# Who makes the sums of the output weights in a Strassen-Winograd feed-forward block: VectorE or GpSimd

## The chip, the cores and the metric

The kernel runs on one core of a Trainium2 chip. The metric is the device time of one execution in microseconds (us). The kernel before takes 2497.96 us, the median of three runs (2496.34 to 2498.91).

In the views of the profile the engines are called PE (TensorE, the matmuls), PEld (its weight loads), DVE (VectorE), ACT (ScalarE), POOL (GpSimd) and SP (SyncE, which here only issues DMAs). PEq, SPq and the like are the sequencers of those engines. Each engine takes its instructions strictly in the order in which they stand in its queue: an instruction that waits holds up all that stand behind it on the same engine.

## The reference

Two layers of an encoder trunk over 1024 prompt tokens and 32 tokens of a running stream, model width 1024, feed-forward width 2816, all in fp32. Layer 0 mixes tokens by a gated linear recurrence (HGRN2), layer 1 by attention over a sliding window. Behind each mixer stands a SwiGLU block with a norm on both sides:

```python
x = x + rms_norm(mix, norm_mix_post[layer])
hf = rms_norm(x, norm_ffn_pre[layer])
a, b = jnp.split(hf @ w_ffn_in[layer], 2, axis=-1)
x = x + rms_norm((jax.nn.silu(a) * b) @ w_ffn_out[layer], norm_ffn_post[layer])
```

The change lies in the last line of it, in the product with `w_ffn_out` and in what is prepared for it while the product with `w_ffn_in` runs.

## The kernel before, in words

Tokens stand in three blocks: block 0 and block 1 of 384 columns, block 2 of 288. Every fp32 product is made of three matmuls on halves in fp32r: a weight tile `wst` arrives by DMA from SP's queue (L91, 512 KB), ACT casts it to the high half `wh` (L102), DVE subtracts to get the low half `wl` (L103), and PE adds high by high, high by low and low by high. There are two buffers for `wst`, so that SP can have a unit's two tiles under way and no more.

**The up projection** (`ffn`, the loop over `j`) has 22 units of 256 output features. Units 0 to 3 are plain. Units 4 to 21 are `fin_7(j)`: for blocks 0 and 1 a Strassen-Winograd scheme with seven products in place of eight, 12 matmuls of 384 columns each (L520), and for block 2 plain products in two halves, 24 matmuls of 288 columns each (`fin_half`, L142); the last two units leave block 2 to later. At the head of a unit `prep(j)` makes four sums of the unit's two weight tiles (L463 to L465, `sr`, `sh`, `sl`), and in it DVE joins the products: `u` is the sum of the first two (L554, called u2 below; it is also what frees the PSUM bank that the second half of block 2 takes), `uk` two further ones, kept in four buffers. SP stores the outcome to `g` in HBM (L380, L570, L576). After each second unit `tpart` makes four sums of activations, and POOL's queue stores them to `t` (L501).

**The sums for the down projection.** The output weights stand in HBM in quarters `wo[0]` to `wo[3]`. `spart(c)` takes a strip of 384 columns of all four (the last strip is 256 wide), and there are 15 strips, called pieces below. Per piece POOL's queue loads four tiles of 192 KB (L484), DVE makes four sums (L485 to L488), and POOL's queue stores them to `sd` (L490). The four tiles have the tags `xo` (two of them, two buffers), `rb2` and `nv` (one buffer each); so a piece's loads wait until the stores of the piece before have landed. The loop asks for piece 0 at unit 5, for the second `tback` (sums of activations of units 0 to 3) at unit 6, and for one piece per unit after that; a scheduler then sets the order on each engine, and since POOL's rows wait for no matmul, its pieces follow each other as fast as they can from unit 6 on.

**The norm's loads.** Behind the last piece the tag `xo` belongs to the norm of the next stage: its loads of the residual stream (L292, `xo<-xsa` in layer 0, `xo<-xsc` in layer 1) stand in SP's queue between the weight loads of the last units, and take the buffers that the pieces use.

**The down projection** runs through a list `PR` of products; each loads six weight tiles (five of 512 KB, one of 256 KB) and the activations to them (L647 and the load ahead of it, tiles `gl` and `gh`), and multiplies (L679). A product can carry a third block along on the same weight tiles (`third`). Between groups of matmuls a table (`s0`, `s1` in `hook`) says how many steps of the norm of block 0 and block 1 are taken. In layer 1 the kernel ends with `put2` for block 2, a sum over partitions on PE (L245, L262) and the last four vector operations (L828, L829) before the output is stored.

Of the kernel before, what the change touches and what calls it, by code (L numbers as in the profile page):

```python
# [8 lines left out]
F32 = mybir.dt.float32  # L9
# [50 lines left out]
def build(nc, tc, I, O):  # L60
# [281 lines left out]
    def ffn(L, nx, post1, post, wmix, v1, w2, xold, wnext, spill, yout, res):  # L342
# [135 lines left out]
        def spart(c):  # L478

            n = slice(c * 384, min(c * 384 + 384, NP2 * 512))  # L480
            w = n.stop - n.start
            a11, a12, a21, a22 = ts = four(w)
            for i, t in enumerate(ts):
                nc.gpsimd.dma_start(t, wo[i][:, n])  # L484
            nc.vector.tensor_tensor(a22, a21, a22, add)  # L485
            nc.vector.tensor_tensor(a21, a11, a21, sub)
            nc.vector.tensor_tensor(a11, a22, a11, sub)
            nc.vector.tensor_tensor(a12, a12, a11, sub)  # L488
            for i, t in enumerate((a22, a11, a21, a12)):
                nc.gpsimd.dma_start(sd[i][:, n], t)  # L490
# [90 lines left out]
        for j in range(NSTD, NF):  # L581
            if j in (NSTD, NSTD + 2):
                tback((j - NSTD) // 2)
            elif pieces:
                spart(pieces.pop(0))
            fin_7(j, j < NF - 2)
        close(spc)
# [38 lines left out]
        if yout is None:  # L626
            PR = [p + (None,) for p in (P1, P6, P2, P7, P4, P5, P3, (A11, E), (A12, F), (A22, F), (A21, E))]
        else:
            PR = [P1 + (E,), P2 + (F,), P6 + (None,), P7 + (None,), P4 + (F,), P5 + (None,), P3 + (None,),
                  (A21, E, None)]  # L630
# [84 lines left out]
        def put2(k, x, more):  # L715

            d = dst(k, 2)
            if yout is None:
                put(k, 2, lambda d: tt_(d, d, x, add) if more else nc.scalar.copy(d, x))
                return None  # L720

            if more:
                tt_(d, d, x, add)
                x = d
            if k < KT - 1:
                sq_acc(accs[2], W, x, k == 0)
                q = None
            else:
                q = tmp()
                nc.scalar.activation(q[:, :W], x, AF.Square)  # L730
            nc.scalar.activation(d, x, AF.Copy, scale=pcol(w2, k))
            return q

        if yout is None:
# [29 lines left out]
            for h in range(2):  # L764
# [5 lines left out]
                for m in M:  # L770
                    put2(4 * h + m, pt[m][:, :W], False)
        else:
# [5 lines left out]
            for m in M:  # L778
                put(m, 0, lambda d: nc.scalar.copy(d, pb[m][:, :384]))
                put2(m, pa[m][:, :W], False)  # L780
# [8 lines left out]
            pb = four_b()  # L789
            product(pa, 384, False, third=(pb, True, True))  # L790
            for m in M:
                put(4 + m, 0, lambda d: tt_(d, Y[:, m, :], pa[m][:, :384], add))
                nc.scalar.copy(dst(4 + m, 2), pb[m][:, :W])

            s0 = {1: 1, 2: 1, 3: 1, 4: 1, 6: 1, 8: 1}
            s1 = {11: 1, 12: 2, 13: 1, 14: 2}
            pa = four_a()
            side[0] = True
            product(pa, 384, True, hook(0, (0, s0)))
            for m in M:  # L800
                put(4 + m, 1, lambda d: tt_(d, d, pa[m][:, :384], add))
            product(pa, 384, False, hook(5, (0, s0)))
            for m in M:
                put(m, 1, lambda d: tt_(d, Y[:, m, :], pa[m][:, :384], add))
            if yout is not None:

                xo = newx(0)[0].bitcast(F32)[:, :, :W]
                nc.sync.dma_start(xo, xold[2])
            pb = four_b()
            side[0] = False  # L810
            product(pb, W, True, hook(10, (0, s0), (1, s1)))
            for m in M:
                q = put2(4 + m, pb[m][:, :W], True)
# [1002 lines left out]
```

## Time and profile before

| what | value |
|---|---|
| median of three runs | 2497.96 us |
| the profiled execution's own time | 2498.63 us |
| its span (first to last instruction in the trace) | 2496.9 us |
| mean granted clock of TensorE | 0.987 |
| busy: PE, DVE, ACT, POOL | 2391.6, 1821.6, 1163.1, 432.6 us |
| units 4 to 21 of layer 0 | 728.0 to 1111.0 us |
| units 4 to 21 of layer 1 | 1837.5 to 2224.0 us |
| down projection of layer 0 | 1123.7 to 1378.7 us |
| down projection of layer 1 | 2236.5 to 2474.3 us |

How to read the views: the first part of the page gives the busy time of each engine and its share of the span. A row of the groups names the line, engine, operation and tiles, then how often, the busy time in us and the mean of one in ns, and behind the last bar how long the engine sat idle just before, and what ended that (`<-`). A row of the timeline begins with the start and the length in us; in brackets stands the idle time before it and its releaser. A row of the windows has, for one stretch, its length and each engine's busy time in us with the number of instructions, then PE's granted clock, the share of time of the DMA engines and GB/s.

### The profile page before, as it was taken

To read this page: it belongs to the slowest core of one execution; us is meant where nothing else is said; L and a number is where in the kernel's file an instruction comes from. 1 tells how busy PE (TensorE), PEld (TensorE's weight loads), DVE (VectorE), ACT (ScalarE), POOL (GpSimd) and SP (SyncE) were. 2 spreads that over 40 slices of the span, in tenths; PEclk is the share of its full clock that TensorE was granted. 3 is DMA by queue.
4 is the path that set the end of the run, shared out by engine and by line. 5 is a ranking of instruction groups with operands and counts; after the bars stand their busy time and mean duration, and the time that the engine had idled before them with its cause. 6 is when DMAs were issued, how large, how long until landed. Compare 5 with 4: busy or idle time off the path is not lost.

```text
span 2496.9 us, 46466 instructions
## 1 busy us (share of the span) xinstructions
PE 2391.6 (96%) x17664; PEld 2314.2 (93%) x17664; DVE 1821.6 (73%) x3989; ACT 1163.1 (47%) x2542; POOL 432.6 (17%) x825
## 2 busy tenths in 40 slices
PE   8999999999999989999999999999999899999996
PEld 8999998998999889999988998778999899999996
DVE  8888789888887677655688747678886676653667
ACT  6655655666533223324556426787432223333543
POOL 4343233230013340000000211000103430000000
PEclk9999999999999999999999999999999999999998
DMA  5332334443434653237677542334426552245655
GB/s 174 103 101 97 121 111 144 125 137 126 152 126 163 218 205 109 94 113 229 211 230 245 183 142 78 104 113 160 147 97 207 199 198 96 87 163 162 205 182 185
DMA packets 159512, 377.34 MB, mean 151 GB/s; under 512 B 20104, under 2 KB 82472, under 8 KB 159288
## 3 DMA queue, kind: packets, MB, share of 16 engines
q1 hardware_dynamic: 137528, 307.77, 38.7%
q0 software_dynamic: 21760, 66.61, 7.8%
q8 instruction: 138, 2.26, 0.4%
q14 instruction: 86, 0.70, 0.1%
HBM read 288.71 MB, written 84.90 MB: 150 GB/s over the span
## 4 chain that ended last, share of the span: by engine, by line
PE 57%; DVE 16%; DMA 12%; issue 6%; ACT 6%; POOL 3%; SPq 0%; DVEq 0%; POOLq 0%; ACTq 0%
PE mm L142 16%; PE mm L520 10%; PE mm L153 7%; PE mm L679 6%; PE c L679 5%; PE c L520 4%; PE mm L164 4%; DVE wl L103 3%; DMA xo<-in_wfo 2%; ACT wh L102 1%; DMA wst<-in_wfo 1%; DMA gl<-t 1%; DMA gl<-g 1%; DMA s<-xo 1%; ACT P L1559 1%
## 5 line engine op out<-in xcount | busy, mean ns | idle before, releaser
L103 DVE TENSOR_TENSOR wl<-wst,wh 128x1024 fp32r<-128x1024 f32 (+1 forms) x323 | 384.6, 1195 | 151.0 <-ACT wh L102 147.0
L142 PE MATMUL mm<-xh,wh 128*128 128x288 f32 (+1 forms) x1344 | 428.8, 320 | 37.8 <-DVE u L554 28.3
L142 PE MATMUL mm<-xh,wl 128*128 128x288 f32 (+1 forms) x1344 | 423.6, 315 | 7.6 <-DVE wl L103 7.6
L142 PE MATMUL mm<-xl,wh 128*128 128x288 f32 (+1 forms) x1344 | 422.9, 315 | 0.5 <-DVE xl L275 0.2
L102 ACT CAST wh<-wst 128x1024 fp32r<-128x1024 f32 (+1 forms) x323 | 328.2, 1021 | 200.0 <-PE mm L520 43.6
L142 PEld LDWEIGHTS mm<-xh,wh 128*128 128x128 f32 x1344 | 258.1, 192 | 43.1 <-DVE u L554 31.2
L142 PEld LDWEIGHTS mm<-xh,wl 128*128 128x128 f32 x1344 | 258.2, 192 | 10.0 <-DVE wl L103 9.8
L142 PEld LDWEIGHTS mm<-xl,wh 128*128 128x128 f32 x1344 | 258.2, 192 | 2.8 <-DVE xl L278 1.2
L153 PE MATMUL mm<-xh,wh 128*128 128x384 f32 (+1 forms) x624 | 206.6, 332 | 0.4 <-DVE rt L236 0.4
L153 PE MATMUL mm<-xh,wl 128*128 128x384 f32 (+1 forms) x624 | 202.7, 325 | 2.2 <-DVE wl L103 1.1
L153 PE MATMUL mm<-xl,wh 128*128 128x384 f32 (+1 forms) x624 | 203.9, 327 | 0.0
L164 PE MATMUL mm<-wh,xh 128*128 128x256 f32 x576 | 166.6, 289 | 0.0
L164 PE MATMUL mm<-wh,xl 128*128 128x256 f32 x576 | 163.2, 283 | 0.0
L164 PE MATMUL mm<-wl,xh 128*128 128x256 f32 x576 | 162.9, 283 | 0.0
L679 PE MATMUL c<-gl,wh 128*128 128x384 f32 (+1 forms) x440 | 143.1, 326 | 3.4 <-DVE gl L647 3.1
L679 PE MATMUL c<-gh,wh 128*128 128x384 f32 (+1 forms) x440 | 141.6, 326 | 3.1 <-ACT gh L646 2.3
L464 ACT CAST sh<-sr 128x512 fp32r<-128x512 f32 x144 | 87.8, 620 | 121.6 <-PE mm L520 94.7
L679 PE MATMUL c<-gh,wl 128*128 128x384 f32 (+1 forms) x440 | 141.7, 323 | 0.0
L647 DVE TENSOR_TENSOR gl<-gl,gh 128x768 fp32r<-128x768 f32 (+3 forms) x111 | 93.5, 845 | 65.7 <-ACT gh L646 65.4
L679 PE MATMUL mm<-gl,wh 128*128 128x384 f32 (+1 forms) x396 | 130.9, 331 | 4.8 <-DVE gl L647 4.7
L679 PE MATMUL mm<-gh,wh 128*128 128x384 f32 (+1 forms) x396 | 128.6, 330 | 5.4 <-ACT gh L646 4.3
L646 ACT CAST gh<-gl 128x768 fp32r<-128x768 f32 (+3 forms) x111 | 82.4, 746 | 102.3 <-DMA gl<-t 44.6
(394 smaller groups left out, 6419.4 us busy)
## 6 DMA issues: line engine op xcount, KB each, us to landing
wst<-in_wfi SPq DMA_DIRECT2D x88, 512.0 KB
wst<-in_wfo SPq DMA_DIRECT2D x55, 512.0 KB
wst<-in_wfq SPq DMA_DIRECT2D x47, 512.0 KB
wst<-s SPq DMA_DIRECT2D x40, 512.0 KB
gl<-t SPq DMA_DIRECT2D x40, 384.0 KB
wst<-in_wi SPq DMA_DIRECT2D x24, 512.0 KB
wst<-in_wg SPq DMA_DIRECT2D x24, 512.0 KB
wst<-in_wao SPq DMA_DIRECT2D x24, 512.0 KB
```

The costliest lines, as they stand in the source:

```text
L102: nc.scalar.copy(wh[:, s], st[:, s])
L103: nc.vector.tensor_tensor(wl[:, s], st[:, s], wh[:, s].bitcast(F32), sub)
L142: last_mm[0] = nc.tensor.matmul(ps[:, :W], w, x, start=i == 0, stop=i == n - 1)
L153: last_mm[0] = nc.tensor.matmul(ps[:, :W], w, x, start=u == k == i == 0, stop=u == 1 and k == 3 and i == 2)
L164: last_mm[0] = nc.tensor.matmul(ps[:rows, :256], x, w, start=i == 0, stop=i == n - 1)
L464: nc.scalar.copy(h, r)
L520: last_mm[0] = nc.tensor.matmul(ps[:, :384], a, c, start=start and k == i == 0, stop=k == 3 and i == 2, skip_group_check=True)
L646: nc.scalar.copy(hs, ls.bitcast(F32))
L647: nc.vector.tensor_tensor(ls, ls.bitcast(F32), hs.bitcast(F32), sub)
L679: last_mm[0] = nc.tensor.matmul(pt[:, :Wt], a, c[:, q, :], start=st and i == groups[0][0] and q == e == 0, stop=sp_ and i == groups[-1][-1 ...
L1559: nc.scalar.activation(P[:rows, pr, pi * o2:pi * o2 + n], sc[:rows, pr, pi], AF.Exp, bias=ng[:rows, hh:hh + 1], scale=0.125, accum_out=rs[ ...
```

## The change

In both layers the four sums of a piece go from DVE to POOL, which already issues the piece's loads and stores. The loads are asked for at the end of the unit before, by `sload`; the sums and the stores stand in `spart` at the head of the next unit. In layer 1 the order of the products in `PR` is another: the product P4 no longer carries the product of `A22` with `F` (block 2) along. In its place the last stage has two products of block 2 alone, `(A22, F)` and `(A21, E)`, added in PSUM. So `A22` is loaded and split a second time, and the copies and additions that joined the two halves of block 2 in SBUF (`put2` with `more`) are gone. The table of the norm's steps is spread over these two products.

```diff
-        def spart(c):
+        terms = []
+
+        def sload(c):
             n = slice(c * 384, min(c * 384 + 384, NP2 * 512))
-            w = n.stop - n.start
-            a11, a12, a21, a22 = ts = four(w)
+            ts = four(n.stop - n.start)
             for i, t in enumerate(ts):
                 nc.gpsimd.dma_start(t, wo[i][:, n])
-            nc.vector.tensor_tensor(a22, a21, a22, add)
-            nc.vector.tensor_tensor(a21, a11, a21, sub)
-            nc.vector.tensor_tensor(a11, a22, a11, sub)
-            nc.vector.tensor_tensor(a12, a12, a11, sub)
+            terms[:] = [n, ts]
+
+        def spart():
+            n, (a11, a12, a21, a22) = terms
+            terms.clear()
+            with after_dense():
+                nc.gpsimd.tensor_tensor(a22, a21, a22, add)
+                nc.gpsimd.tensor_tensor(a21, a11, a21, sub)
+                nc.gpsimd.tensor_tensor(a11, a22, a11, sub)
+                nc.gpsimd.tensor_tensor(a12, a12, a11, sub)
             for i, t in enumerate((a22, a11, a21, a12)):
                 nc.gpsimd.dma_start(sd[i][:, n], t)
...
-            elif pieces:
-                spart(pieces.pop(0))
+            elif terms:
+                spart()
             fin_7(j, j < NF - 2)
+            if j != NSTD + 1 and pieces:
+                sload(pieces.pop(0))
...
-            PR = [P1 + (E,), P2 + (F,), P6 + (None,), P7 + (None,), P4 + (F,), P5 + (None,), P3 + (None,),
-                  (A21, E, None)]
+            PR = [P1 + (E,), P2 + (F,)] + [p + (None,) for p in (P6, P7, P4, P5, P3, (A22, F), (A21, E))]
...
-            pb = four_b()
-            product(pa, 384, False, third=(pb, True, True))
+            product(pa, 384, False)
             for m in M:
                 put(4 + m, 0, lambda d: tt_(d, Y[:, m, :], pa[m][:, :384], add))
-                nc.scalar.copy(dst(4 + m, 2), pb[m][:, :W])
...
-            pb = four_b()
-            side[0] = False
-            product(pb, W, True, hook(10, (0, s0), (1, s1)))
+            product(pa, W, True, hook(10, (0, s0), (1, s1)))
+            product(pa, W, False, hook(15, (0, s0), (1, s1)))
             for m in M:
-                q = put2(4 + m, pb[m][:, :W], True)
+                q = put2(4 + m, pa[m][:, :W])
```

The order of the instructions that a scheduler made of it differs at three places.

POOL, one piece in the middle of layer 1's up projection. `in_wfo1` are the output weights, `s1_0` to `s1_3` the stored sums. Before:

```order
L484 DMA nv_23785<-in_wfo1 128x384
L484 DMA xo_23782<-in_wfo1 128x384
L484 DMA xo_23784<-in_wfo1 128x384
L484 DMA rb2_23783<-in_wfo1 128x384
L490 DMA s1_0_21516<-nv_23785 128x384
L490 DMA s1_2_21518<-xo_23784 128x384
L490 DMA s1_1_21517<-xo_23782 128x384
L490 DMA s1_3_21519<-rb2_23783 128x384
```

And in the changed kernel, whose lines are shifted by a few:

```order
L485 DMA nv_23785<-in_wfo1 128x384
L485 DMA xo_23782<-in_wfo1 128x384
L485 DMA xo_23784<-in_wfo1 128x384
L485 DMA rb2_23783<-in_wfo1 128x384
L493 TENSOR_TENSOR nv_23785<-xo_23784,nv_23785 128x384
L494 TENSOR_TENSOR xo_23784<-xo_23782,xo_23784 128x384
L498 DMA s1_0_21516<-nv_23785 128x384
L495 TENSOR_TENSOR xo_23782<-nv_23785,xo_23782 128x384
L498 DMA s1_2_21518<-xo_23784 128x384
L496 TENSOR_TENSOR rb2_23783<-rb2_23783,xo_23782 128x384
L498 DMA s1_1_21517<-xo_23782 128x384
L498 DMA s1_3_21519<-rb2_23783 128x384
```

The sums stand between the loads and the stores of their own piece; the loads of the next piece stand behind the last store, and no load of it stands ahead of a sum of this one.

SP, where it goes from the weight tiles of unit 13 (`wst_24466` is the second of them) to those of unit 14 (`wst_24688`, `wst_24694`). `xo<-xsc0` are the norm's loads. Before:

```order
L91 DMA wst_24466<-in_wfi1 128x1024
L91 DMA wst_24688<-in_wfi1 128x1024
L380 DMA g1_21_21511<-tmp_24164 128x288
L570 DMA g1_01_21507<-uk_24080 128x384
L91 DMA wst_24694<-in_wfi1 128x1024
L576 DMA g1_11_21509<-uk_24082 128x384
L292 DMA xo_28101<-xsc0_93 128x384
L91 DMA wst_24905<-in_wfi1 128x1024
L380 DMA g1_20_21510<-tmp_24392 128x288
L292 DMA xo_28103<-xsc0_93 128x384
```

And in the changed kernel:

```order
L91 DMA wst_24466<-in_wfi1 128x1024
L292 DMA xo_27931<-xsc0_93 128x384
L292 DMA xo_27933<-xsc0_93 128x384
L91 DMA wst_24688<-in_wfi1 128x1024
L380 DMA g1_21_21511<-tmp_24164 128x288
L578 DMA g1_01_21507<-uk_24080 128x384
L91 DMA wst_24694<-in_wfi1 128x1024
L584 DMA g1_11_21509<-uk_24082 128x384
L91 DMA wst_24905<-in_wfi1 128x1024
```

The norm's two loads went ahead of unit 14's weight tiles, one past five rows of the queue, the other past seven. They take the two `xo` buffers of the last piece, and each waits for that piece's store from its buffer to land. Layer 0 has the same two rows at the same place, as `xo<-xsa`.

DVE, around u2 of unit 12 (`u_24307`); `sr_24700` is the first sum of unit 14's weight tiles, `nv_25782` and `xo_25781` belong to piece 13. Before:

```order
L485 TENSOR_TENSOR nv_25782<-xo_25781,nv_25782 128x384
L574 TENSOR_TENSOR uk_24082<-uk_24082,u_24081 128x384
L486 TENSOR_TENSOR xo_25781<-xo_25779,xo_25781 128x384
L497 TENSOR_TENSOR acc_24217<-uk_24082,uk_23865 128x384
L487 TENSOR_TENSOR xo_25779<-nv_25782,xo_25779 128x384
L498 TENSOR_TENSOR uk_23863<-acc_24217,uk_23863 128x384
L499 TENSOR_TENSOR acc_24218<-uk_24080,acc_24217 128x384
L554 TENSOR_TENSOR u_24307<-mm_24294,tmp_24292 128x384
L465 TENSOR_TENSOR sl_24492<-sr_24490,sh_24491 128x512
L463 TENSOR_TENSOR sr_24700<-wst_24688,wst_24694 128x512
```

And in the changed kernel:

```order
L582 TENSOR_TENSOR uk_24082<-uk_24082,u_24081 128x384
L505 TENSOR_TENSOR acc_24217<-uk_24082,uk_23865 128x384
L506 TENSOR_TENSOR uk_23863<-acc_24217,uk_23863 128x384
L507 TENSOR_TENSOR acc_24218<-uk_24080,acc_24217 128x384
L463 TENSOR_TENSOR sr_24700<-wst_24688,wst_24694 128x512
L562 TENSOR_TENSOR u_24307<-mm_24294,tmp_24292 128x384
L465 TENSOR_TENSOR sl_24492<-sr_24490,sh_24491 128x512
L463 TENSOR_TENSOR sr_24706<-sr_24700,wst_24688 128x512
```

The piece's sums are gone from the queue, and the first sum of unit 14's weights now stands ahead of u2 of unit 12. Layer 0 has these two rows in the same order as well.

More of the change, by code (lines that the diff above doesn't have):

```diff
@@ L713, in hook, with put2 @@
             return f
-        def put2(k, x, more):
+        def put2(k, x):
             d = dst(k, 2)
             if yout is None:
-                put(k, 2, lambda d: tt_(d, d, x, add) if more else nc.scalar.copy(d, x))
+                put(k, 2, lambda d: nc.scalar.copy(d, x))
                 return None
-            if more:
-                tt_(d, d, x, add)
-                x = d
             if k < KT - 1:
@@ L770, in ffn @@
                 for m in M:
-                    put2(4 * h + m, pt[m][:, :W], False)
+                    put2(4 * h + m, pt[m][:, :W])
         else:
@@ L779, in ffn @@
                 put(m, 0, lambda d: nc.scalar.copy(d, pb[m][:, :384]))
-                put2(m, pa[m][:, :W], False)
+                put2(m, pa[m][:, :W])
             pb = four_b()
@@ L788, in ffn @@
                 tt_(dst(4 + m, 1), Y[:, m, :], pa[m][:, :384], add)
-            pb = four_b()
-            product(pa, 384, False, third=(pb, True, True))
+            product(pa, 384, False)
             for m in M:
                 put(4 + m, 0, lambda d: tt_(d, Y[:, m, :], pa[m][:, :384], add))
-                nc.scalar.copy(dst(4 + m, 2), pb[m][:, :W])
-            s0 = {1: 1, 2: 1, 3: 1, 4: 1, 6: 1, 8: 1}
-            s1 = {11: 1, 12: 2, 13: 1, 14: 2}
+            s0 = {1: 1, 2: 1, 3: 1, 5: 1, 7: 1, 9: 1}
+            s1 = {12: 1, 13: 1, 14: 1, 15: 1, 16: 1, 17: 1}
+            pb = four_b()
+            product(pb, 384, True, hook(0, (0, s0)))
+            for m in M:
+                put(4 + m, 1, lambda d: tt_(d, d, pb[m][:, :384], add))
+            product(pb, 384, False, hook(5, (0, s0)))
+            for m in M:
+                put(m, 1, lambda d: tt_(d, Y[:, m, :], pb[m][:, :384], add))
+            xo = newx(0)[0].bitcast(F32)[:, :, :W]
+            nc.sync.dma_start(xo, xold[2])
             pa = four_a()
             side[0] = True
-            product(pa, 384, True, hook(0, (0, s0)))
+            product(pa, W, True, hook(10, (0, s0), (1, s1)))
+            product(pa, W, False, hook(15, (0, s0), (1, s1)))
             for m in M:
[L801 to L808, printed above, removed]
-            pb = four_b()
-            side[0] = False
-            product(pb, W, True, hook(10, (0, s0), (1, s1)))
-            for m in M:
-                q = put2(4 + m, pb[m][:, :W], True)
+                q = put2(4 + m, pa[m][:, :W])
         close(gpc)
```

## The prediction

> **What bounds the kernel now.** The page first, for the shares.
>
> ```profile
> span 2496.9 us, 46466 instructions
> PE 2391.6 (96%) x17664; PEld 2314.2 (93%) x17664; DVE 1821.6 (73%) x3989; ACT 1163.1 (47%) x2542; POOL 432.6 (17%) x825
> L142 PE MATMUL mm<-xh,wh 128*128 128x288 f32 (+1 forms) x1344 | 428.8, 320 | 37.8 <-DVE u L554 28.3
> ```
>
> PE is the bound over the whole, 96%. Its largest idle time behind one releaser stands in the third row: 28.3 us before L142, ended by DVE's u2. That is the place of the change. The waits of PE from unit 6 on, first in layer 1 (1880 to 2050), then in layer 0 (770 to 930), say how it is spread:
>
> ```profile
> PE mm L142 <- DVE u L554: 15.7, 5, 7.1
> ```
> ```profile
> PE mm L142 <- DVE u L554: 12.6, 4, 5.8
> ```
>
> Nine stops, all at u2, all while pieces run. What they cost with all their effects comes out of the windows (length, PE, PEld, DVE, ACT, POOL, clock):
>
> ```profile
> 728.00:1111.00 383.00, 370.35 (x2284) 369.00 (x2283) 263.09 (x456) 108.74 (x173) 79.54 (x148) 0.98 0.44 146
> 1837.50:2224.00 386.50, 370.84 (x2284) 369.25 (x2283) 261.45 (x454) 106.58 (x170) 79.54 (x148) 0.98 0.43 144
> 1950.00:2000.00 50.00, 45.12 (x273) 44.48 (x273) 34.14 (x64) 12.85 (x21) 19.48 (x37) 0.97 0.60 205
> 2050.00:2200.00 150.00, 150.00 (x945) 150.00 (x944) 101.59 (x169) 46.96 (x73) 8.59 (x16) 1.00 0.30 101
> ```
>
> The last row is the stage with all pieces done: PE full, 945 matmuls in 150 us. A unit has 84 + 48 = 132 of them: 132 x 150/945 = **20.95 us**. The matmuls of 384 columns follow each other by 0.1737 us (16 steps from 1876.79 to 1879.57, below), so the 84 take 14.6 and the 48 the rest, 6.35, or 0.132 each. Units 4 to 21, two of them without block 2, should take 16 x 20.95 + 2 x 14.6 = 364.4 us. They take 383.0 and 386.5: **18.6 us lost in layer 0, 22.1 in layer 1**, stops and a clock of 0.97 behind them. That is all that a change of the sums can win here.
>
> Why the stops: one piece follows the next, and DVE's queue holds the piece's sums ahead of u2. The start of unit 6 of layer 1 (`c` at 1879.39), the first store of pieces 1 and 2, that of piece 13, and where PE goes on in unit 12:
>
> ```profile
> 1876.79 0.33 PE L520 MATMUL mm<-xh,wh 128*128 128x384 f32 x1
> ...
> 1879.39 0.33 PE L520 MATMUL c<-xh,wh 128*128 128x384 f32 x1
> 1879.57 0.33 PE L520 MATMUL c<-xl,wh 128*128 128x384 f32 x1
> ```
> ```profile
> 1892.66 0.55 POOL L490 DMA_DIRECT2D s<-nv  x1 [3.18 <-DVE nv L485]
> ...
> 1904.57 0.54 POOL L490 DMA_DIRECT2D s<-nv  x1 [0.52 <-DVE nv L485]
> ```
> ```profile
> 2033.96 0.55 POOL L490 DMA_DIRECT2D s<-nv  x1 [2.13 <-DVE nv L485]
> ```
> ```profile
> 2037.00 0.61 PE L142 MATMUL mm<-xh,wh 128*128 128x288 f32 x1 [1.95 <-DVE u L554]
> ```
>
> Twelve pieces in 2033.96 - 1892.66 = 141.3 us: **11.78 us a piece**, whatever PE does. In the order of before, a sum of piece 13 stands ahead of u2 of unit 12. PE can reach that u2's bank 6 x 20.95 + 11.5 us after the start of unit 6 (six units; then four products of 12 and a half of block 2, 48 x 0.1737 + 24 x 0.132), so at 137.2. Piece 13's first sum ends, with its store, at 2033.96 - 1879.39 = 154.6; the sums that follow and u2 take until 157.6, where PE goes on (2037.00). The difference, 20.4 us, is nearly all of the 22.1. So the pieces, not PE, set the pace from unit 6 to unit 12, and I forecast by the same account.
>
> **The sums on POOL.** 120 sums leave DVE (0.558 us each, first row) and come to POOL. POOL made none of 128x384 in this stage; the nearest rows are its sums of that shape elsewhere:
>
> ```profile
> L485 DVE TENSOR_TENSOR nv<-xo,nv x30: 424/558/560, 695.6 to 2043.0; 128x384 f32<-128x384 f32 x28, 128x256 f32<-128x256 f32 x2
> ```
> ```profile
> L1386 POOL TENSOR_TENSOR ra<-ra,tmp 128x384 f32<-128x384 f32 x10 | 10.6, 1056 | 0.0
> L1385 POOL TENSOR_TENSOR ra<-ra,tmp 128x384 f32<-128x384 f32 x10 | 10.3, 1029 | 77.5 <-DVE tmp L1383 45.3 <-DVE rs L1562 26.0 <-issue 6.2
> L1377 POOL TENSOR_TENSOR sinr<-sinr,rb 128x384 f32<-128x384 f32 x4 | 5.4, 1351 | 0.0
> ```
>
> I take 1.03 us; the bound above is 1.35, and below 0.558, as if POOL were as fast as DVE.
>
> The sums stand in one queue with the loads and stores, so a piece is now a chain: the load that waited for the last piece's store lands, four sums, two store issues among them (0.54 each, as in the POOL rows above), the store lands, and so on. The DMAs' times from issue to landing:
>
> ```profile
> xo<-in_wfo POOLq DMA_DIRECT2D x56, 192.0 KB, 3.7
> s<-xo POOLq DMA_DIRECT2D x56, 192.0 KB, 2.3
> ...
> rb<-in_wfo POOLq DMA_DIRECT2D x28, 192.0 KB, 2.7
> ...
> s<-nv POOLq DMA_DIRECT2D x28, 192.0 KB, 2.1
> ```
> ```profile
> DMA to landing us min/median/max: 2.3/3.6/6.9
> ```
>
> The second fence is of the loads of layer 1's pieces alone. By medians: 3.7 + 4 x 1.03 + 2 x 0.54 + 2.3 = **11.2 us a piece**. By the shorter landings of the other two tiles (2.7, 2.1), which I take for a time with little else under way: 10.0. With sums of 1.35: 12.5; with sums of 0.558, 9.3. So by the likeliest of these a piece gets hardly shorter than 11.78: what DVE's queue cost in waiting, POOL's slower sums cost in work.
>
> **Where it bites now.** No DVE row waits for a piece any more. Two other rows do. One is u2's neighbour u3 of unit 12: it takes a `uk` buffer whose store to `t` stands in POOL's queue behind piece 13, about as late as before. The other binds harder. The norm's two loads (L292) stand in SP's queue ahead of unit 14's first weights, and wait for the stores of the **last** piece. Behind them stand unit 14's tiles; `prep(14)`'s first sum waits for those, and stands ahead of u2 of unit 12 on DVE; and that u2 holds PE's bank. In the trace of before SP already stands there, from 2034.16 to 2046.80, but with two further units of weights taken in, so PE did not see it:
>
> ```profile
> 2034.16 0.32 SPq L576 DMA_DIRECT2D g<-uk  x1
> 2046.80 0.32 SPq L292 DMA_DIRECT2D xo<-xsc  x1
> 2047.90 0.33 SPq L91 DMA_DIRECT2D wst<-in_wfi  x1
> ```
>
> The sum, in us from the start of unit 6, with c for a piece: piece 1's first sum starts at 1892.66 - 0.55 - 1879.39 = 12.7 (its loads wait for activations' sums that are not changed); piece 14's at 12.7 + 13c, and three stores to `t` in between add 3 x 0.54 = 1.6; three sums and a store issue until the second `xo` store starts (the last strip is narrower) 3.9; landing 2.4; then SP issues and unit 14's two tiles land, 1.1 us to the first issue (2046.80 to 2047.90 above) and 5 for 1 MB at the 205 GB/s of the window at 1950; sr and u2, 0.7 + 0.55. PE stood since 137.2, so it loses 12.7 + 13c + 1.6 + 3.9 + 2.4 + 6.1 + 1.25 - 137.2 = **13c - 109**. While SP is blocked the other DMAs run out, and the last five pieces should go at 10.0; with eight at 11.2 the mean c is 10.75 and the loss 30.7; with eight at 11.8 it is 35. I take 33, plus 2 for the clock behind a long stop (0.97 for 50 us in the row above): 35 a layer, 70 for both, in place of 18.6 + 22.1 = 40.7. **Added: 29 us.** Bounds: all pieces at 10.0, 21 a layer, +1; sums at 1.35 give 12.5 and 11.3, a mean of 12.0, 47 + 2 a layer, +57; sums at 0.558 give 9.3 and 8.1, a mean of 8.8, 6 a layer, -29.
>
> **The down projection of layer 1.** PE's count is the same: 132 matmuls of 288 move from beside P4 to a product of their own. Added are six weight tiles with their casts, 1.02 us on ACT and 1.20 on DVE each by these rows, so 6 and 7 us on engines that stand at 107 and 137 busy of 238 there (windows); gone are four copies and four sums.
>
> ```profile
> L103 DVE TENSOR_TENSOR wl<-wst,wh 128x1024 fp32r<-128x1024 f32 (+1 forms) x323 | 384.6, 1195 | 151.0 <-ACT wh L102 147.0
> ...
> L102 ACT CAST wh<-wst 128x1024 fp32r<-128x1024 f32 (+1 forms) x323 | 328.2, 1021 | 200.0 <-PE mm L520 43.6
> ```
> ```profile
> 2236.50:2474.30 237.80, 234.30 (x1458) 231.53 (x1457) 136.76 (x185) 107.03 (x152) 0.00 (x0) 1.00 0.61 193
> ```
>
> What a product of 288 columns takes by itself against what PE needs:
>
> ```profile
> 1291.46:1378.70 87.24, 77.39 (x536) 72.86 (x536) 71.33 (x111) 52.02 (x90) 5.26 (x4) 0.98 0.73 232
> 2453.87:2474.27 20.40, 18.98 (x135) 17.79 (x134) 16.00 (x27) 8.96 (x15) 0.00 (x0) 1.00 0.44 136
> ```
>
> The first are layer 0's four such products, 21.8 each; the second the last product of before, 20.4. 132 x 0.132 is 17.4. So the second product costs 3 to 4 more than beside P4. Against that the end gets shorter:
>
> ```profile
> 2477.11 1.01 DVE L309 TENSOR_TENSOR mix<-mix,xo 128x384 f32<-128x384 f32 x2
> 2478.04 1.17 DVE L723 TENSOR_TENSOR mix<-mix,c 128x288 f32<-128x288 f32 x3
> ...
> 2483.43 0.15 DVE L250 COPY small<-mm 32x1 f32<-32x1 f32 x1 [2.44 <-PE mm L245]
> ```
>
> The norm of block 1 keeps DVE until 2478.1, four us behind the last matmul (the end of both windows that close at 2474.3), and only then come the additions of block 2. With 20 us more of matmuls behind P3 the norm's steps are done earlier, and the additions are gone: from the last matmul about 0.8 for the last square, 2.4 for L245's matmuls, and from 2483.43 on as before, 13.5, to 2496.9. That is 16.7 in place of 22.6: -6. Net **-2.5**, bounds -6 (the second product hidden) and +4 (weights bound both products, and the norm still late).
>
> **Sum.** 2498.63 of the profiled execution + 29 - 2.5 = 2525.1; that execution lies 0.7 above the median, so about **2525 us**, slower by 1.1%.
>
> **The rivals.** First, the stops vanish: the pieces get ahead of PE, from c = 109/13 = 8.4 down, and neither row is ever late. For it: DVE's waits for pieces are gone, and they were the only releaser named. Against: POOL alone is busy 8 x 0.54 + 4 x 1.03 = 8.4 in a piece, and waits for landings besides. It would give 2498.6 - 40.7 - 2.5 = 2455. Second, as before: only the store to `t` binds, at a cycle near 11.5, 12c - 121 = 17 a layer by the account that gave 20.4 (12 x 11.78 - 121); 2498.6 - 7 - 2.5 = 2489, up to 2496 with c of 11.8. That needs SP's two loads to pass unseen, against their place in the queue. Third, no change by balance: the loss is 13c - 109 at c = 10.0 to 10.2, 21 to 23.6 a layer: 2497 to 2502. Fourth, the far side: POOL's and DVE's sums hold each other up, since DVE is 68% busy in the window at 1950 (34.14 of 50). The trace has one such row, a POOL sum of 288 columns that took 1.78 where the one ahead of it took 0.81, while DVE's L103 (mean 1.20) took 1.69:
>
> ```profile
> 1556.86 0.81 POOL L1385 TENSOR_TENSOR ra<-ra,tmp 128x288 f32<-128x288 f32 x1 [13.99 <-DVE tmp L1383]
> 1557.63 1.78 POOL L1386 TENSOR_TENSOR ra<-ra,tmp 128x288 f32<-128x288 f32 x1
> ```
> ```profile
> 1557.06 1.69 DVE L103 TENSOR_TENSOR wl<-wst,wh 128x1024 fp32r<-128x1024 f32 x1
> ```
>
> One sum in three held up by 1 us makes 1.36 of the mean 1.03, the bound above: +57, 2553; each layer's DVE work would then also stretch, up to 2560. The Trainium skill has this as a rule, SBUF — State Buffer (section "SBUF: two separate sides"): a VectorE operation with two SBUF inputs and a GpSimd operation that reads SBUF share ports that one of them holds for its whole instruction. The row agrees; that the 20 sums of 384 columns in L1385 and L1386 have means of 1.03 and 1.06 says that it does not strike each time.
>
> **Chances.** My forecast (2508 to 2542) 0.52; the far side 0.2; balance 0.12; as before 0.06; stops gone 0.10. What a measurement of this kernel can tell is about 0.2%, 5 us. Faster is stops gone and most of "as before": 0.15; same is 0.08 of balance and 0.01 of "as before": 0.09; slower the rest of balance, the forecast and the far side: 0.76. The range goes from 2490 to 2560: below lie the stops gone, above a worse lock.
>
> **What the changed profile would show.** In each layer one stop of PE of 25 to 40 us at L142 in unit 12, ended by DVE's u2 (now L562), in place of four or five short ones; SP standing at the norm's `xo` loads from unit 10 or 11 on until the last store `s<-xo` has landed; POOL's sums at 1.0 to 1.1 us and first stores `s<-nv` 10 to 12 us apart; units 4 to 21 at about 399 us each; behind the last matmul no L308 or L309 and some 17 us to the end. I am wrong in the mechanism if PE's stop has another releaser or several stops remain, in the size if the pieces are under 10.0 or over 12.5 us apart, and in the last part if the last two products take over 44 us.

## The result, and the profile after

The changed kernel takes **2571.05 us** (median of four, 2566.54 to 2572.84) against 2497.15 before on the same chip (2493.33 to 2498.91): a ratio of 1.0289, 95% interval 1.0274 to 1.0304. That is slower, as forecast, but by 74 us where 27 were forecast, and above the range of 2490 to 2560.

Where the time went, from the starts and ends of the same matmuls in the two traces (the profiled execution after has a span of 2567.8 us, 70.9 more than before):

| stretch | before, us | after, us | difference |
|---|---|---|---|
| layer 0, unit 4 to the first matmul of the down projection | 395.5 | 435.6 | +40.1 |
| layer 0, down projection | 255.0 | 254.5 | -0.5 |
| from there to unit 4 of layer 1 | 458.8 | 462.2 | +3.4 |
| layer 1, unit 4 to the first matmul of the down projection | 399.1 | 432.1 | +33.0 |
| layer 1, down projection | 237.7 | 241.0 | +3.3 |
| from the last matmul of it to the end | 22.6 | 14.4 | -8.2 |

The page of the changed kernel, as before:

```profile
span 2567.8 us, 46367 instructions
PE 2393.6 (93%) x17664; PEld 2314.2 (90%) x17664; DVE 1812.4 (71%) x3871; ACT 1169.6 (46%) x2544; POOL 557.9 (22%) x945
...
L142 PE MATMUL mm<-xh,wh 128*128 128x288 f32 (+1 forms) x1344 | 424.5, 316 | 84.6 <-DVE u L562 75.7
```

PE's work is the same. The idle time before L142 behind DVE's u2 went from 28.3 to 75.7 us. PE's waits around the up projection, layer 0 first, then layer 1 (total, times, longest):

```profile
PE mm L142 <- DVE u L562: 37.0, 2, 34.9
PE mm L528 <- DVE uk L569: 9.6, 1, 9.6
PE mm L528 <- DVE uk L566: 5.4, 1, 5.4
```
```profile
PE mm L142 <- DVE u L562: 38.7, 2, 37.8
PE mm L528 <- DVE uk L569: 7.5, 1, 7.5
PE mm L528 <- DVE uk L566: 2.1, 1, 2.1
```

Four or five short stops have become one of 35 to 38 us and three short ones. The long one in layer 1, in the timelines of SP, DVE and PE:

```profile
2035.63 0.33 SPq L91 DMA_DIRECT2D wst<-in_wfi  x1
2100.14 1.50 SPq L292 DMA_DIRECT2D xo<-xsc  x2
2101.75 0.41 SPq L91 DMA_DIRECT2D wst<-in_wfi  x1
...
2103.23 0.80 SPq L91 DMA_DIRECT2D wst<-in_wfi  x1
```
```profile
2110.69 0.69 DVE L463 TENSOR_TENSOR sr<-wst 128x512 f32<-128x512 f32 x1 [37.86 <-DMA wst<-in_wfi]
2111.30 0.55 DVE L562 TENSOR_TENSOR u<-mm,tmp 128x384 f32<-128x384 f32 x1
```
```profile
2111.91 0.61 PE L142 MATMUL mm<-xh,wh 128*128 128x288 f32 x1 [37.81 <-DVE u L562]
```

Read upwards: PE waits for u2; u2 stands behind `sr`, for which DVE waited 37.86 us; `sr` waits for weights that SP issued at 2101.75 and 2103.23; and SP, which had issued nothing since 2035.63, came to these only when the norm's loads `xo<-xsc` went out at 2100.14. What those waited for is in POOL's timeline, the last piece:

```profile
2095.23 0.72 POOL L493 TENSOR_TENSOR nv<-xo,nv 128x256 f32<-128x256 f32 x1 [1.04 <-DMA xo<-in_wfo]
...
2097.95 0.57 POOL L498 DMA_DIRECT2D s<-xo  x1
...
2099.21 0.56 POOL L498 DMA_DIRECT2D s<-xo  x1
```

The pieces' first stores in layer 1 run from 1938.87 to 2086.79 for thirteen, 12.33 us apart; in layer 0 from 786.30 to 940.62, 12.86 apart. One piece of layer 1 whole, to the next one's first sum:

```profile
2025.61 0.99 POOL L493 TENSOR_TENSOR nv<-xo,nv 128x384 f32<-128x384 f32 x1 [2.46 <-DMA xo<-in_wfo]
2026.68 1.00 POOL L494 TENSOR_TENSOR xo<-xo 128x384 f32<-128x384 f32 x1
2027.62 0.57 POOL L498 DMA_DIRECT2D s<-nv  x1
2028.21 1.03 POOL L495 TENSOR_TENSOR xo<-nv,xo 128x384 f32<-128x384 f32 x1
2029.16 0.56 POOL L498 DMA_DIRECT2D s<-xo  x1
2029.75 1.03 POOL L496 TENSOR_TENSOR rb<-rb,xo 128x384 f32<-128x384 f32 x1
2030.70 0.56 POOL L498 DMA_DIRECT2D s<-xo  x1
2031.27 0.54 POOL L498 DMA_DIRECT2D s<-rb  x1
2031.80 0.54 POOL L485 DMA_DIRECT2D nv<-in_wfo  x1
2032.33 0.54 POOL L485 DMA_DIRECT2D xo<-in_wfo  x1
2033.13 0.54 POOL L485 DMA_DIRECT2D xo<-in_wfo  x1 [0.25 <-DMA s<-xo]
...
2038.82 1.00 POOL L493 TENSOR_TENSOR nv<-xo,nv 128x384 f32<-128x384 f32 x1 [3.99 <-DMA xo<-in_wfo]
```

Sums and the stores between them take 5.09 us (2025.61 to 2030.70), the store's landing until the load of its buffer 2.43 (to 2033.13), that load's landing 5.69 (to 2038.82): 13.2 in this piece. No engine is full in it; it is a chain.

At the end of the kernel the trace shows what was forecast: no L308 or L309 stands behind the last matmul, and L245 follows it at once, at 2553.45 (no bracket, so no idle time ahead of it):

```profile
2553.45 0.76 PE L245 MATMUL mm<-ones,acc 128*128 128x1 f32 x6
...
2557.51 1.57 PE L262 MATMUL mm<-tmp,ones 128*128 128x128 f32 x6 [2.61 <-DVE tmp L261]
```

### The profile page after: what moved, and what is told of

Same layout as the page of the kernel before. It is cut to its first block, busy times and chain, and to the rows that moved or that the text cites. A ratio compares the mean times of both kernels' runs of the same rounds, so it can differ in the third digit from the quotient of the medians.

```text
span 2567.8 us, 46367 instructions
## 1 busy us (share of the span) xinstructions
PE 2393.6 (93%) x17664; PEld 2314.2 (90%) x17664; DVE 1812.4 (71%) x3871; ACT 1169.6 (46%) x2544; POOL 557.9 (22%) x945
## 4 chain that ended last, share of the span: by engine, by line
PE 56%; DVE 15%; DMA 13%; POOL 7%; ACT 5%; issue 4%; SPq 0%; POOLq 0%; DVEq 0%; ACTq 0%
PE mm L142 15%; PE mm L528 10%; PE mm L153 6%; PE mm L688 6%; PE c L688 5%; PE mm L164 4%; PE c L528 4%; DMA xo<-in_wfo 3%; DVE wl L103 3%; DMA wst<-in_wfo 2%; ACT wh L102 1%; DMA wst<-in_wfi 1%; POOL s L498 1%; POOL xo L494 1%; POOL nv L493 1%
## 5 line engine op out<-in xcount | busy, mean ns | idle before, releaser
L142 PE MATMUL mm<-xh,wh 128*128 128x288 f32 (+1 forms) x1344 | 424.5, 316 | 84.6 <-DVE u L562 75.7
L103 DVE TENSOR_TENSOR wl<-wst,wh 128x1024 fp32r<-128x1024 f32 (+1 forms) x329 | 400.3, 1221 | 139.9 <-ACT wh L102 138.7
L142 PE MATMUL mm<-xh,wl 128*128 128x288 f32 (+1 forms) x1344 | 419.9, 313 | 6.4 <-DVE wl L103 6.3
L102 ACT CAST wh<-wst 128x1024 fp32r<-128x1024 f32 (+1 forms) x329 | 334.1, 1020 | 197.4 <-PE mm L528 42.1
L142 PE MATMUL mm<-xl,wh 128*128 128x288 f32 (+1 forms) x1344 | 419.1, 312 | 0.5 <-DVE xl L278 0.3
L142 PEld LDWEIGHTS mm<-xh,wh 128*128 128x128 f32 x1344 | 254.7, 190 | 88.2 <-DVE u L562 77.0
L142 PEld LDWEIGHTS mm<-xh,wl 128*128 128x128 f32 x1344 | 254.9, 190 | 9.3 <-DVE wl L103 9.3
L142 PEld LDWEIGHTS mm<-xl,wh 128*128 128x128 f32 x1344 | 254.9, 190 | 2.5 <-DVE xl L278 1.3
L688 PE MATMUL c<-gl,wh 128*128 128x384 f32 (+1 forms) x484 | 160.0, 331 | 4.1 <-DVE gl L656 3.8
L688 PE MATMUL c<-gh,wh 128*128 128x384 f32 (+1 forms) x484 | 158.4, 330 | 2.9 <-ACT gh L655 2.2
L688 PE MATMUL c<-gh,wl 128*128 128x384 f32 (+1 forms) x484 | 158.1, 328 | 0.0
L656 DVE TENSOR_TENSOR gl<-gl,gh 128x768 fp32r<-128x768 f32 (+3 forms) x117 | 97.8, 839 | 74.3 <-ACT gh L655 72.9
L463 DVE TENSOR_TENSOR sr<-wst 128x512 f32<-128x512 f32 x72 | 57.2, 794 | 127.1 <-DMA wst<-in_wfi 127.1
```

The lines of the kernel that those rows point to most:

```text
L102: nc.scalar.copy(wh[:, s], st[:, s])
L103: nc.vector.tensor_tensor(wl[:, s], st[:, s], wh[:, s].bitcast(F32), sub)
L142: last_mm[0] = nc.tensor.matmul(ps[:, :W], w, x, start=i == 0, stop=i == n - 1)
L463: nc.vector.tensor_tensor(r, x, y, op)
L656: nc.vector.tensor_tensor(ls, ls.bitcast(F32), hs.bitcast(F32), sub)
L688: last_mm[0] = nc.tensor.matmul(pt[:, :Wt], a, c[:, q, :], start=st and i == groups[0][0] and q == e == 0, stop=sp_ and i == groups[-1][-1 ...
```

## The experiments

Twelve runs in three groups, each group beside the kernel before on its own chip, whose medians were 2492.68, 2490.60 and 2491.84 us. The kernels are compared by the ratio to it, and the difference stands in us.

| kernel | median, us | ratio, 95% interval | against before, us |
|---|---|---|---|
| the change | 2571.05 | 1.0289 (1.0274 to 1.0304) | +73.9 |
| sums on POOL alone | 2566.94 | 1.0300 (1.0282 to 1.0318) | +74.3 |
| order of products alone | 2490.12 | 0.9987 (0.9973 to 1.0002) | -2.6 |
| norm's loads in own tiles | 2525.80 | 1.0127 (1.0110 to 1.0144) | +33.1 |
| norm's loads behind the weights | 2520.88 | 1.0118 (1.0103 to 1.0133) | +29.0 |
| half sums | 2522.50 | 1.0124 (1.0086 to 1.0161) | +31.9 |
| no sums | 2521.75 | 1.0121 (1.0088 to 1.0153) | +31.2 |
| no sums, norm's loads behind | 2465.96 | 0.9896 (0.9876 to 0.9916) | -25.9 |
| sums on DVE, loads a unit ahead | 2488.24 | 0.9985 (0.9972 to 0.9997) | -3.6 |
| sums on DVE, one piece per unit | 2450.78 | 0.9831 (0.9817 to 0.9846) | -41.9 |
| the same again | 2454.56 | 0.9852 (0.9829 to 0.9875) | -36.0 |
| sums on POOL, two pieces per pair of units | 2452.20 | 0.9840 (0.9814 to 0.9866) | -38.4 |
| sums on DVE, one per unit, products of before | 2454.09 | 0.9847 (0.9831 to 0.9863) | -37.8 |

### Which half of the change

The two halves apart. First the sums alone; its edit is the first part of the diff above, with the down projection left as before.

> The change of the sums alone, in both layers; the down projection of layer 1 is that of before. By the theory (the added time is the pieces' chain on GpSimd, which keeps SyncE at the norm's loads and PE at u2 of unit 12) it keeps all of the loss and lacks the 5 us that the end of layer 1 won by the traces (+3.3 in the down projection, -8.3 behind it): 2576 us (2570 to 2582), with one stop of PE of about 35 us at u2 in unit 12 of each layer. The rival, that the new order of products in layer 1 is what costs, expects 2500 us or less.

Then the order of products alone, with `spart` on VectorE as before.

> The other half alone: the sums are made on VectorE as before, and layer 1's down projection has the two products of block 2 at its end. Theory: 2492 us (2488 to 2496), the down projection 241 us in place of 237.7 and 14.4 us from the last matmul to the end in place of 22.6. Rival (the second product is bound by its weights, and the two effects cancel): 2495 to 2500.

The sums alone cost 74.3 us and the whole change 73.9: the sums are all of the loss. The time itself, 2566.94, lies below the 2570 to 2582 expected, but so does the kernel before on that chip (2492.68 against 2497.15); what the expectation adds to the 2497.15, 79 us, stands at the upper end of the measured interval (70 to 79). The stops are those of the change (36.2 and 36.7 us at u2).

The order of products gives 2.6 us with an interval from 6.7 us faster to 0.5 slower, so a gain is likely and not certain. From the last matmul to the end its trace has 14.6 us (2470.8 to 2485.4), as expected; the down projection ahead of it took 244.7 us there, not the 241 expected.

### Whether SyncE's queue is the way from the pieces to PE

Two ways of taking the norm's loads out of the way. One gives them tiles of their own:

```diff
-                xo = tt("xo", 2) if more is None or k % 5 < 2 else more()
+                xo = tt("xo", 2) if more is None else more()
...
-                                 lambda: mp.tile([128, 384], F32, tag="xo", name="xo", bufs=3), bank=nbank)
+                                 lambda: mp.tile([128, 384], F32, tag="xo", name="xo", bufs=5), bank=nbank)
```

> The changed kernel, but the norm's loads of the residual behind the up projection take five buffers of their own instead of two of the pieces' and three of their own, so that they no longer wait for the last piece, and stand later in SyncE's queue. Theory: the long stop at u2 of unit 12 goes, and what is left is the wait of u3 of unit 12 for the store to t behind piece 13, 12c - 121 by the prediction's account, which with the measured c of 12.4 and 12.9 is 28 and 34 us in place of 55 and 59 lost: 2571 - 52 = 2519 us (2505 to 2535). Rival (the pieces on GpSimd slow PE and VectorE down by themselves, and SyncE's rows only stand beside it): above 2555.

It won 41 us of the 74 (33.1 left). But tiles and queue had both changed, so the second keeps the tiles and moves the rows alone, behind a store of the last unit; the queues of VectorE and GpSimd stay as they are in the change.

```diff
-                nc.sync.dma_start(xo[:, :W], xold[:, k, :])
+                with nullcontext() if more is None else tc.issue_after(last_sp[0].ins):
+                    nc.sync.dma_start(xo[:, :W], xold[:, k, :])
...
-            nc.sync.dma_start(gd[0][j % 2][:, j // 2, :], u3)
+            last_sp[0] = nc.sync.dma_start(gd[0][j % 2][:, j // 2, :], u3)
```

> The changed kernel with one thing moved: in SyncE's queue the norm's loads behind the up projection stand behind a store of the last unit, in the same tiles; VectorE's and GpSimd's queues are those of the changed kernel row for row. Theory: as with the norm's loads in their own tiles, 2525 us (2515 to 2532): the stop at u2 of unit 12 goes, the waits of u3 and u7 for stores to t remain (some 25 us in each layer). Rival (the own tiles did it, not the place in the queue): above 2550.

+29.0 in place of +73.9: **the place of two loads in SyncE's queue costs 45 us.** PE's waits in its layer 1:

```profile
PE mm L531 <- DVE uk L569: 15.1, 2, 12.1
PE mm L531 <- DVE uk L572: 8.8, 1, 8.8
PE mm L142 <- DVE u L565: 1.9, 1, 1.9
```

The long stop at L142 is gone. What is left is the other barrier that the prediction names, u3 behind a store to `t`, and a third one, u7 (L572 here, L569 in the change) behind the store of another buffer to `t`: 25.8 us in layer 1.

### What sets the length of the pieces

Half of each sum left out, which leaves half of the sums of the output weights wrong and every load and store in place:

```diff
+                h = (n.stop - n.start) // 2
+                b11, b12, b21, b22 = [t[:, :h] for t in (a11, a12, a21, a22)]
-                nc.gpsimd.tensor_tensor(a22, a21, a22, add)
+                nc.gpsimd.tensor_tensor(b22, b21, b22, add)
...
```

> The changed kernel with the four sums of a piece made over the left half of its columns only (the right half is left out), loads and stores as they are. By the account 13c - 109 per layer, with c shorter by four times half a sum (4 x 0.53 = 2.1 us, from 12.4 and 12.9 measured): 27 us less in each layer, 54 in all, so 2571 - 54 = 2517 us (2505 to 2530), pieces 10.3 and 10.8 us apart. Rival (the chain is not set by the sums; loads and stores take the time that is freed): above 2545.

The pieces come 11.09 us apart in layer 0 and 10.97 in layer 1 (12.86 and 12.33 in the change). By 13 times the difference, 23 and 18, this is 41 us; measured against the kernel before it is +31.9 in place of +73.9, so 42. The factor 13 of the prediction's account holds. The pieces themselves did not come out as expected (10.8 and 10.3): they got 1.8 and 1.4 us shorter, not 2.1, and one reason is that a sum of half the columns took 0.61 to 0.78 us on the mean, not 0.53.

Then all sums left out, so that what was loaded is stored:

```diff
-            with after_dense():
-                nc.gpsimd.tensor_tensor(a22, a21, a22, add)
...
```

> The changed kernel with the four sums of a piece left out, so that what was loaded is stored. Pieces 8 to 8.6 us apart, 13c - 109 at or below 3: no stop of PE at u2 of unit 12, 2571 - 113 = 2458 us (2450 to 2470). Rival (SyncE's wait for the last piece is not what holds PE, or traffic alone slows PE): above 2490.

**This missed**: 2521.75, no faster than with half of the sums. Both theories as written were wrong about it. The profile shows the pieces 7.9 us apart in layer 1 (1903.95 to 2006.62 for fourteen) and yet a stop of 30 us, in the same timelines of SP, DVE and PE:

```profile
2009.39 0.82 SPq L292 DMA_DIRECT2D xo<-xsc  x2
2010.26 0.50 SPq L573 DMA_DIRECT2D g<-uk  x1
2010.87 0.39 SPq L91 DMA_DIRECT2D wst<-in_wfi  x1
```
```profile
2016.26 0.69 DVE L463 TENSOR_TENSOR sr<-wst 128x512 f32<-128x512 f32 x1 [36.61 <-DMA wst<-in_wfi]
```
```profile
2017.48 0.61 PE L142 MATMUL mm<-xh,wh 128*128 128x288 f32 x1 [29.94 <-DVE u L557]
```

It is the same chain, with the weights of unit 12 in place of unit 14: the order of this kernel has the norm's loads between the two weight loads of unit 12, and PE stops in unit 10. The scheduler, which takes the pieces to be done sooner, put the rows that wait for them further ahead. So the account is right for one order and says nothing about another. With the place held as in the experiment above and the sums left out:

> The same with the sums left out. Without them the pieces went 7.9 us apart, but the scheduler then put the norm's loads two units further ahead in SyncE's queue, where they again waited for the last piece, and PE lost 30 us in each layer at u2 of unit 10. With the place held behind the weights nothing is late: no stop over 2 us in units 6 to 20, 2452 us (2446 to 2468). Rival (30 us were lost to the pieces' traffic): above 2500.

2465.96, inside the 2446 to 2468 expected, though with a stop of 7.2 us in layer 0 and 4.2 in layer 1 at u3 that had not been (a store to `t` behind the pieces). The traffic of the pieces is the same as in the run before it, and 57 us are gone: it was the order, not the traffic.

### Whether it is GpSimd, or the pace

The call order asks for a piece per unit; VectorE's queue before has more, with the sums of 2, 3, 2, 2, 2 and 2 pieces ahead of u2 of units 7 to 12. Loads a unit ahead, sums on VectorE:

```diff
-            with after_dense():
-                nc.gpsimd.tensor_tensor(a22, a21, a22, add)
+            nc.vector.tensor_tensor(a22, a21, a22, add)
...
```

> The changed kernel, loads asked for a unit ahead, but the four sums on VectorE. Theory: the call order does not set the queues, the scheduler does, and its VectorE queue has five pieces in two units as before: 2491 us (2485 to 2498), PE's stops at u2 as before. Rival (loads a unit ahead help as such): below 2475.

It is 3.6 us faster than before, no more than the order of products can account for (2.6 by itself, with the interval above); VectorE's queue has the pieces as before, and PE has nine stops at u2 (14.2 and 13.5 us), as before. Asking for the loads a unit ahead did nothing by itself.

Now the pace is made real: VectorE's sums of a piece stand behind the last VectorE row of the unit before (with the new order of products).

```diff
-            tt_(u7, u7, u4, mult)
+            last_u[0] = tt_(u7, u7, u4, mult)
...
-            nc.vector.tensor_tensor(a22, a21, a22, add)
+            with tc.issue_after(last_u[0].ins):
+                nc.vector.tensor_tensor(a22, a21, a22, add)
...
```

> The sums on VectorE as before, but each piece's four sums are put behind the last VectorE row of the unit before, so that one piece stands in each unit where before there were five in two; the new order of products is kept. Theory: the 18.6 and 22.1 us lost before come only from sums that stand ahead of u2 earlier than their loads can be there; with 20.95 us for each piece of 11.8 us nothing waits: 2498 - 41 - 5 = 2452 us (2446 to 2468), PE without a stop of over 1 us in units 6 to 20. Rival (the loss comes from the pieces' traffic or from VectorE's load, whatever the order): above 2480.

2450.78 us: **41.9 us faster than before**, with the new order of products in it (the same pace with the products of before, below, wins 37.8). And with the sums on GpSimd at the same pace, each piece behind the stores to `t` of the last pair of units:

```diff
-                nc.gpsimd.dma_start(td[i][:, k, :], t)
+                last_t[0] = nc.gpsimd.dma_start(td[i][:, k, :], t)
...
-            with after_dense():
+            with tc.issue_after(last_t[0].ins):
                 nc.gpsimd.tensor_tensor(a22, a21, a22, add)
...
```

> The changed kernel with the sums on GpSimd as in it, but each piece's sums stand behind the stores to t of the last pair of units, which wait for VectorE: so two pieces go with two units, 25 us of chain in 41.9 us, and the last piece is in unit 20. The norm's loads then stand behind the weights of the last unit in SyncE's queue. Theory (not GpSimd's sums cost the time, but a queue that runs ahead and the SyncE rows ordered by a last piece that comes too late): no stop of over 2 us in units 6 to 20, 2453 us (2447 to 2468), within 10 us of the sums on VectorE at one per unit. Rival (sums on GpSimd cost time by themselves, by holding up VectorE or by their length): above 2480.

> The kernel with VectorE's sums at one piece per unit again, on the chip of the run before this one, to set the two engines side by side: 2451 us (2447 to 2456).

2452.20 on GpSimd and 2454.56 on VectorE, side by side: their intervals overlap. In neither does the list of PE's waits have an entry in these stretches. The windows from 1880 to 2160, VectorE's kernel first, then GpSimd's (length, PE, PEld, DVE, ACT, POOL, clock):

```profile
1880.00:2160.00 280.00, 280.00 (x1762) 280.00 (x1762) 207.30 (x362) 85.67 (x132) 72.81 (x136) 1.00 0.50 167
```
```profile
1880.00:2160.00 280.00, 280.00 (x1762) 280.00 (x1761) 208.06 (x309) 85.09 (x134) 121.33 (x180) 1.00 0.48 164
```

PE is full in both. So sums on GpSimd do not cost the time of the change, and on VectorE they do not cost it either: the pace does, and with it the place of the norm's loads, which in both paced kernels go out behind all weights of the up projection.

Last, the order of products priced without the stops: the paced sums on VectorE with the products of before.

> VectorE's sums at one piece per unit with the products of before, so that against 2450.8 and 2454.6 us it prices the new order of products without the stops: by the traces (+3.3 in the down projection, -8.3 behind it) it is 5 us slower than with the new order, 2457 us (2453 to 2462). Rival: no difference, 2451 to 2454.

2454.09, ratio 0.9847, between the two runs of the same kernel with the new order (0.9831 and 0.9852). No difference can be told; the 5 us expected are at most partly there.

## Why the prediction was right in its mechanism and wrong in its size

**What bounds, and what can be won.** Right: the account put 18.6 and 22.1 us of loss on the pieces, 40.7 in all, and the paced kernels win 36 to 42 with no stop left. The first rival's price (2455 when the stops vanish) is what they measure, though by a way that the prediction did not name.

**The place.** Right in the main: one long stop of PE at L142 in unit 12 of each layer, ended by u2, with SyncE at the norm's loads until the last store has landed; and moving those two loads alone took 45 us off. The prediction expected 25 to 40 us for the stop, it was 34.9 and 37.8. It named one other row, u3 of unit 12, and passed over u7 of unit 11 (L569), which waits for a store to `t` behind the pieces too: 9.6 and 7.5 us. u3 stopped PE already in unit 10 (5.4 and 2.1). These stops come earlier on the same way: PE is the later at the last barrier, and waits there the less. Still, "several stops remain" was one of the prediction's own signs of a wrong mechanism, and three short ones did remain in each layer, up to 9.6 us.

**The length of a piece: the step that failed.** The prediction had 11.2 us for eight pieces and 10.0 for the last five, 10.75 on the mean. Measured between first sums: 12.94 in layer 0 and 12.43 in layer 1 (by first stores 12.86 and 12.33, the first of them beyond the 12.5 that the prediction named as a sign of a wrong size). Its three terms, over the twelve intervals, against what was put in:

| term | forecast | layer 0 | layer 1 |
|---|---|---|---|
| first sum to the store of the second `xo` | 5.2 | 5.51 | 5.45 |
| that store to the second `xo` load of the next piece | 2.3 | 3.17 | 2.81 |
| that load to the next first sum | 3.7 | 4.26 | 4.17 |

The sums were nearly right. The two landing terms failed, and not by their usual size: the medians of the twelve links are 2.4 us for the second term in both layers and 3.8 and 4.0 for the third, close to the 2.3 and 3.7 put in. But a chain adds up every link, the long ones too, so it goes by the mean. The second term reached 3.4 to 5.1 us, mostly where a store landed late or where three stores to `t` stood between; the third reached 7.0 us in layer 0 and 5.7 in layer 1. The long landings are those beside SyncE's weights: of the 30 second `xo` loads in this trace, the 7 that had a weight load issued between 4 us ahead of them and 1 us ahead of their landing took 5.3 us on the mean, the 23 others 3.4. That this traffic is the cause was not tested.

So the first eight pieces took 13.5 and 12.9 us on the mean, not 11.2. The last five in layer 1 took 11.3 (11.35, 11.19, 12.09, 11.33 and 10.45), not 10.0, though SyncE issued nothing from 2035.96 to 2100.14 and the DMA engines were busy for 0.43 and 0.44 of the time (2040 to 2060 and 2060 to 2095). The 2.7 us that had been taken for "little else under way" is the landing of `rb`, which in the trace of before shared its time with 1.4 other loads of the pieces on the mean, an `xo` tile with 2.3; in the changed kernel `rb` takes 3.7 itself.

With the measured c the account holds. 13c - 109 is 59 in layer 0 and 53 in layer 1; unit 6 starts at 769.93 and 1922.30, PE was to reach u2's bank 137.2 us later, and goes on at 964.30 and 2111.91, so 57.2 and 52.4 late. The forecast had 33 for each. These two differences, 24 and 19, are nearly all of the 44 us by which the forecast of the up projections fell short (29 added, 73 measured). The terms beside c were each a little off: SyncE to u2's end took 10.3 us (2101.64, the end of the norm's loads, to 2111.91) against 7.35, and the stores to `t` were counted on top of a c that has them in it; these two work against each other, so that the account comes so close is in part luck.

**The clock.** Forecast 2 us a layer behind the long stop. The stages lost 58.7 and 55.1 us by the count of before (18.6 + 40.1 and 22.1 + 33.0), and PE was 57.2 and 52.4 late at its last stop, so 1.5 and 2.7 were lost behind it. Right.

**The far side.** The fourth rival had 2553, up to 2560, for sums stretched to 1.35. That mechanism is there (the last section), but it is the smaller part: the sums took 1.04 to 1.16 us on the mean, so four of them 0.25 us more than the 4 x 1.03 put in. The time went beyond even this rival by the landings.

**The down projection of layer 1.** Right within its size: forecast 3 to 4 us more for the second product and 6 less behind it, net -2.5; the traces have +3.3 and -8.2, net -4.9, and the run of this half alone -2.6 with an interval that reaches to no change. The two traces compared here show the smallest loss of all: over the eleven traces with the new order the down projection takes 241.0 to 246.5 us, over the three with the old one 237.4 to 237.9, and behind its last matmul 13.8 to 14.6 against 22.4 to 22.6. The last two products took 40.1 us, under the 44 that the prediction named as its sign.

The 3.4 us between layer 0's down projection and unit 4 of layer 1, where nothing was changed, is not explained by any run; over all fourteen traces this stretch goes from 458.0 to 462.2 us.

## What to carry to other kernels

In a queue that issues in order, a transfer that waits for a late buffer costs what stands behind it in its queue, not what it carries: look in the order for rows that moved ahead of weight loads, and price the stop from the moment that their buffer comes free. A chain of load, sum and store through single buffers goes by the landing of the last transfer of each burst, and its length by the mean of all links, the long ones in it; a median over transfers leaves those out (here 2.4 and 3.8 us for the two landings by median, 3.17 and 4.26 on the mean, in layer 0). When work that nobody needs soon runs ahead of its consumer, hold it to the consumer's pace by an edge on its own queue before giving it another engine: that won 36 to 42 us here, with the sums on either engine.

## What the runs showed of the hardware

Sums on GpSimd stretched those of VectorE's operations that read two SBUF tiles while such a sum ran, and not those with an operand in PSUM. VectorE's groups from 1880 to 2160 in the two paced kernels, VectorE's sums first, then GpSimd's:

```profile
L465 DVE TENSOR_TENSOR sl<-sr,sh 128x512 fp32r<-128x512 f32 x53 | 36.3, 684 | 0.5 <-ACT sh L464 0.5
L103 DVE TENSOR_TENSOR wl<-wst,wh 128x1024 fp32r<-128x1024 f32 x26 | 31.7, 1221 | 11.6 <-ACT wh L102 11.6
...
L463 DVE TENSOR_TENSOR sr<-sr,wst 128x512 f32<-128x512 f32 x13 | 8.9, 688 | 0.2
L559 DVE TENSOR_TENSOR uk<-mm,u 128x384 f32<-128x384 f32 x14 | 7.8, 557 | 14.5 <-PE mm L521 14.5
```
```profile
L465 DVE TENSOR_TENSOR sl<-sr,sh 128x512 fp32r<-128x512 f32 x54 | 40.5, 751 | 5.3 <-ACT sh L464 5.2
L103 DVE TENSOR_TENSOR wl<-wst,wh 128x1024 fp32r<-128x1024 f32 x27 | 39.5, 1464 | 7.4 <-ACT wh L102 7.4
...
L463 DVE TENSOR_TENSOR sr<-sr,wst 128x512 f32<-128x512 f32 x13 | 13.9, 1072 | 0.0
...
L566 DVE TENSOR_TENSOR uk<-mm,u 128x384 f32<-128x384 f32 x14 | 7.7, 554 | 3.0 <-PE mm L528 3.0
```

L103 went from 1.22 to 1.46 us and L465 from 0.68 to 0.75, L463's sum of `sr` and `wst` from 0.69 to 1.07, while the row with an operand in PSUM (`mm`) kept 0.55. These are means of rows that met a sum and rows that did not. One stretch of GpSimd's kernel, VectorE first, then GpSimd:

```profile
2083.77 1.22 DVE L103 TENSOR_TENSOR wl<-wst,wh 128x1024 fp32r<-128x1024 f32 x1 [0.56 <-ACT wh L102]
...
2088.59 0.56 DVE L576 TENSOR_TENSOR uk<-uk,mm 128x384 f32<-128x384 f32 x1 [2.73 <-PE mm L528]
...
2089.76 2.30 DVE L103 TENSOR_TENSOR wl<-wst,wh 128x1024 fp32r<-128x1024 f32 x1
```
```profile
2088.39 1.02 POOL L495 TENSOR_TENSOR xo<-nv,xo 128x384 f32<-128x384 f32 x1
...
2089.94 1.03 POOL L496 TENSOR_TENSOR rb<-rb,xo 128x384 f32<-128x384 f32 x1
```

The L103 beside which no sum ran took 1.22 us, the one that met a sum 2.30, and L576 with its operand in PSUM met a sum and kept 0.56. In the whole window the 6 rows of L103 that overlap a GpSimd sum took 2.31 us on the mean, the 21 others 1.22, and none of these over 1.23. VectorE has 53 rows fewer in the window and is busy 0.8 us longer (208.06 against 207.30): moving 30 us of sums away freed nothing. Here it hid in VectorE's slack. The rule of the Trainium skill's page SBUF — State Buffer (section "SBUF: two separate sides"), that the two engines exclude each other for such operations, agrees with these rows.
